# Results written back into their operands' pages, an unscaled first chunk and a new order of steps in a two-layer hybrid encoder

## The chip, the cores and the metric

The kernel runs on one core of a Trainium2 chip. Its engines each work through a list of instructions in the order in which the program gives them: TensorE (PE) multiplies matrices, its weight loads are PEld; VectorE (DVE), ScalarE (ACT) and GpSimd (POOL) do the elementwise work; SyncE (SP) issues nearly all transfers, and ACT a few. Matrix results land in PSUM banks, from where ACT or DVE must copy them before a bank can be used again. The metric is the device time of one execution in microseconds; lower is better. The kernel before takes 1392.69 us (median of three runs, 1391.5 to 1395.56).

## The reference

Two layers over 1024 new frames (eight tiles of 128 rows) and, with the same weights, 32 later frames (a ninth tile) that also read caches. In each layer:

```
h = rmsnorm(x, norm_g);  z = h @ w_in          # 1024 -> 2976 columns, cut into
(a_q, a_k, a_v, a_g,  b_cq, b_ckv, b_kr, b_g,  c_q, c_k, c_v, c_g) = split(z)
ret  = retention(rope(a_q), rope(a_k)/8, a_v)             # 4 heads, chunk by chunk, with a state
q    = [rmsnorm, rope(rmsnorm)] of rmsnorm(b_cq) @ w_uq   # latent attention (MLA), 8 heads of 96
k, v = rmsnorm(b_ckv) @ w_ukv, and one rotated key part for all heads
mla  = softmax(q k^T / sqrt(96), causal by chunks of 64) v
band = softmax(rms(c_q) rms(c_k)^T / 8 + bias[clip(distance)]) c_v   # last 8 chunks and own
mix  = [rmsnorm(ret)*silu(a_g), mla*silu(b_g), band*silu(c_g)]
y    = x + mix @ w_out
```

The outputs are y of both groups and, per layer, the retention state, the normalised latents and the normalised band keys and values.

## The kernel before, in words

Every product that feeds the results is made from two float32r parts, hi and lo: `whi` and `wlo` of a weight, `H_94` (hi) and `H_95` (lo) of the transposed input, and three matmuls (hi*hi, hi*lo, lo*hi) stand for one.

**Pages.** SBUF is cut into 60 pages of 128x512 float32 (`N_PAGES`, L40). `page()` takes the one that has been free longest, `free()` gives it back. Work beside the main line is written as tasks (Python generators): `prep` (input of a tile), `b` (latent attention's q, k, v of a tile), `ret`, `bk`, `bq`, `band`, `smp`, `mla`. A task takes its next step when its input is there, when a clock that the planner keeps has passed its due time (`GAPS`), and when `safe()` finds pages enough for all tasks that have begun (`NEED`, `MOST`, `STREAMS` per kind). So the tables of numbers at the top set the order in which the program is written; a scheduler then orders the instructions of each engine within these dependencies.

**Stages of a layer.** `layer_in` projects the 1024 columns in eleven steps, in the order of `STEPS`: "b" (416 columns), and then 256 columns at a time. The steps ag, bg0, bg1, cg are gates (`gates`), the others run tile by tile (`chunk`): 24 matmuls of one tile into a bank `pj` (there are two), which `unload` copies into a page `z`. The weights of a step are fetched a step ahead. Band attention of two tiles (`band_attn`) runs beside the gates: `band_score` makes 128 rows against up to five key tiles in two banks `s` (there are three), adds the bias, takes the maximum and the exponential (pages `bs` and `bPA`); `transposed` turns the probabilities through banks `ps` (three) into pages `PT`; `values` multiplies them with v. Then come 64 units of latent attention (`mla`: score, transpose, values), beside which the two halves of the output product (`out_part`) run at the rates `RATES`; the second begins no earlier than `STARTS[1]`.

**The start.** In the first layer x comes in transposed already (`xt`, two halves of 256 KB a tile), and the row norm is applied after the product: `first_prep` splits `xt` in `H`, squares it, sums the squares over its columns by a matmul with ones (`s<-ones,xsq`) and takes the power -0.5 (`rstd`, result `r0`). `unload` scales by `r0` as it copies a bank, so a bank waits for the norm of its tile. The tile t=1 is loaded on ACT's queue, all else on SP's. `misc_task` writes the flipped position bias 128 times into DRAM (`bt`, 768 KB, for both layers) and loads it again in slanted rows (`braw`, `braws`).

Of the kernel before, what the change touches and what calls it, by code (L numbers as in the profile page):

```python
# [39 lines left out]
FETCH_B = 20  # L40
E2 = "G"
STEPS = ("b", "ak", "cv", "ck", "av", "aq", "bg0", "cq", "ag", "cg", "bg1")
CAP = 16
AHEAD_U = 8
NEED_W = dict(b=17, u=16)
# [13 lines left out]
MOST = dict(prep=2, misc=2, b=5, ret=4, bk=2, bq=7, band=7, smp=3, mla=4)  # L59
MARGIN = 0  # L60
STREAMS = dict(prep=3, misc=1, b=2, ret=2, bk=1, bq=1, band=2, smp=1, mla=1)
BANKS = dict(ps=3, s=3, pj=2)
# [28 lines left out]
class Task:  # L91


    def __init__(self, kind, gen, when):
        self.kind, self.gen, self.when = kind, gen, when
        self.ready, self.held, self.started = 0.0, 0, False


class Kern:
# [167 lines left out]
    def may(self, task):  # L267
        return self.safe(max(0, min(MOST[task.kind], NEED[task.kind] - task.held)), task)

# [3 lines left out]
    def step_task(self, task):  # L273
        task.started = True
        self.cur, last = task, self.cur
        try:
            with self.urgent(URGENT.get(task.kind, 0)):
                next(task.gen)
# [177 lines left out]
    def prep(self, t, xh, hT):  # L456
        n = 128 if t < 8 else NS
        xn = [self.page([512], name="xn") for _ in range(2)]
        ss = self.st(2)
        for j in range(2):  # L460
            self.act(xn[j][:n], xh[j][:n], AF.Square, scale=1.0 / 32, accum_out=ss[:n, j:j + 1])
# [9 lines left out]
        self.free(*xh)  # L471
        yield
        for j in range(2):
            p = self.bank((4, 128), "prep")
            for i in range(4):
                self.tr(p[:, i, :n], xn[j][:n, 128 * i:128 * i + 128])
            self.parts(t, j, p[:, :, :n], hT)
        self.free(*xn)
        self.prepped.add(t)
        yield  # L480

    def first_prep(self, t, hT):
# [4 lines left out]
        for j in range(2):  # L487
            (self.nc.scalar if t == 1 else self.nc.sync).dma_start(
                xt[j], (A["xt_p"][t] if t < 8 else A["xt_s"])[:, 4 * j:4 * j + 4])
        yield  # L490
        for j in range(2):
            self.parts(t, j, xt[j], hT, LO0[j])
        yield
        for x in xt:
# [11 lines left out]
        self.free(sq)  # L506
        self.prepped.add(t)
        yield
# [15 lines left out]
    def new_hT(self):  # L524
        self.prepped = set()
# [32 lines left out]

    def unload(self, t, p, W, z=None):

        if z is None:
            z = self.page([W], name="z")
        with self.urgent(URGENT_Z):
            if t < 8:
                self.act(z, p, **({} if self.rb is None else dict(scale=self.r0[:, t:t + 1])))
            elif self.rb is None:
                self.unstack(z[:NS], p)
# [6 lines left out]

    def b_task(self, l, t, z):
        A = self.A
        n = 128 if t < 8 else NS
        ss = self.st(3)
        sq = self.page([416], name="sq")
# [17 lines left out]
        self.free(z, sq, kr)  # L597
        yield
# [67 lines left out]
    def q_task(self, l, t, n, ch, cl):  # L666
        for c in range(2):
# [12 lines left out]
            yield  # L680
            qn = self.page([4, 96], name="qn")
            rp = self.page([2, 4, 32], name="rp")
# [9 lines left out]
            else:  # L692
                self.qs[c] = qn
            self.free(rp, zq, sq)
            yield

    def kv_task(self, l, t, n, ch, cl, kr):
# [3 lines left out]
        for c in range(2):  # L701
            p = self.bank((4, 128), "b")
            self.latent(p, ch, cl, [(2, self.W["u"][4 + c])])
            zk = self.page([4, 64], name="zk")
            self.unstack(zk[:n], p[:, :, :64])
# [6 lines left out]
            yield  # L712
            kt = self.page([4, 96], name="kt")
            self.tt(kt[:n, :, :64], zk[:n], r[:n].unsqueeze(2).to_broadcast([n, 4, 64]), OP.mult)
            self.free(zk, sq)
            self.nc.gpsimd.tensor_copy(kt[:n, :, 64:], kr[:, None, :].to_broadcast([n, 4, 32]))
# [203 lines left out]
    def ret_task(self, l, t, zk, zq):  # L920
# [4 lines left out]
        tmp = self.page([2, 4, 2, 32], name="rt")  # L925
        rx = self.page([8, 64], name="rx")
        for j, src in enumerate((zq, zk)):
# [8 lines left out]
        self.free(zq)  # L936
        ro = self.page([8, 2, 32], name="ro")
        self.tt(ro[:n, :, 0], zz[:, :, 0], tm[:, :, 1], OP.subtract)
        self.tt(ro[:n, :, 1], zz[:, :, 1], tm[:, :, 0], OP.add)
        xz = (self.xz if t < 8 else self.xzs)[:n].unsqueeze(2).to_broadcast([n, 8, 64])  # L940
        self.tt(rx[:n], ro[:n].rearrange("p h a d -> p h (a d)"), xz, OP.mult)
        self.free(z, tmp, ro)
        yield
# [112 lines left out]
    def band_k_task(self, l, t, z):  # L1056
# [12 lines left out]
        self.free(z, sq)  # L1069
        if t >= 4:  # L1070
# [56 lines left out]
    def band_prep(self, l, pr):  # L1127
# [27 lines left out]
        for j in range(2):  # L1155
# [6 lines left out]
            self.bqt[2 * pr + j] = (qh, ql)  # L1162
        yield

    def band_attn(self, l, pr):
        b0 = 2 * pr
        yield from self.band_prep(l, pr)
        for b in (b0, b0 + 1):
            q = self.bqt.pop(b)
            PT, sums = [], self.st(4)  # L1170
            for h in range(4):
                P = self.band_score(h, b, q, sums[:, h:h + 1])
                yield
                PT.append(self.transposed(P))
                yield
            o = self.bank((2, 128), "o")
            for hp in range(2):
                self.values(o[:, hp], [(k, self.bv[k][:, 128 * hp:128 * hp + 128])
                                       for k in range(max(0, b - 4), b + 1)], PT[2 * hp:2 * hp + 2])
            p = self.inverse_rows(sums, 2)  # L1180
            mx = self.mixboth(3, b)
            self.put_mix((6, 7), (b,), mx, p)
            self.tt(mx, o, mx, OP.mult)
            yield
            self.bfull = b + 1
            self.free(*q)
# [4 lines left out]

    def band_score(self, h, b, q, so):

# [4 lines left out]
        m = self.st(2)  # L1198
        t = self.page([128 * nb], name="bs")
        sB = self.bank((128 * x + 128,), "s")  # L1200
# [255 lines left out]
    def layer_in(self, l, hT):  # L1456
# [12 lines left out]
        def cb_b(t, p):  # L1469
            self.spawn("b", self.b_task(l, t, self.unload(t, p, 416)), lambda: "u" in self.W)  # L1470
            if t == MISC_T:
# [41 lines left out]
        for name, nxt in zip(STEPS, STEPS[1:] + (None,)):  # L1513
# [5 lines left out]
            for _ in gen(name):  # L1519
# [3 lines left out]
                self.poll()  # L1523
                self.press(lambda: len(self.fg) > CAP or not self.safe(2))
            for x, _ in todo:
# [27 lines left out]
    def run(self):  # L1553
# [17 lines left out]
        self.poll()  # L1571
        self.load(self.tab, A["tab"])
        self.load_layer(0)
        x_of = src_p
        for l in range(DEPTH):
# [33 lines left out]
            for x, _ in enumerate(self.mla(l)):  # L1609
                self.poll()  # L1610
                self.press(lambda: not self.safe(6))
                for i in range(2):
# [67 lines left out]
```

## Time and profile before

| | |
|---|---|
| time, median of 3 runs | 1392.69 us (1391.5 to 1395.56) |
| profiled execution | 1385.13 us, span of the profile 1383.3 us |
| PE busy | 1327.4 us (96%) in 10339 matmuls |
| DVE, ACT, POOL busy | 845.3, 760.5 and 458.9 us (61%, 55%, 33%) |
| the chain that ended last | PE 79%, DMA 7%, ACT 4%, DVE 4%, POOL 4% |
| transfers | 130.56 MB, 94 GB/s over the span |

The busy share of an engine is the time in which it has an instruction in it; PE's instructions overlap, so 96% does not say that PE ran at its peak. The granted clock of PE (PEclk) is given as a share of its full speed: 1.00 is 2.4 GHz, 0.50 is 1.2 GHz. A row of the timeline begins with its start and its duration in us; what stands in brackets behind it is how long the engine had been idle and what ended that.

### The profile page before, as it was taken

The numbers are of one execution on the slowest core, as the hardware profiler recorded it, in microseconds if no ns is written. First come the engines' busy times: TensorE is split into PE (matmuls) and PEld (weight loads), VectorE is DVE, ScalarE is ACT, GpSimd is POOL, SyncE is SP. The second block draws the span as 40 slices with busy tenths as digits, with TensorE's granted clock in tenths as the row PEclk, the third lists the DMA queues.
The fourth block names the chain that finished last, engine by engine and source line by source line (L and its number), as shares of the span: only waits on it lengthen the run. The fifth ranks groups of instructions, "written<-read, shape, count | busy, mean of one in ns | idle before, by whom it ended". The sixth has DMA issues, their size and how long they took to land.

```text
span 1383.3 us, 28562 instructions
## 1 busy us (share of the span) xinstructions
PE 1327.4 (96%) x10339; PEld 1214.6 (88%) x10339; DVE 845.3 (61%) x2558; ACT 760.5 (55%) x2180; POOL 458.9 (33%) x686
## 2 busy tenths in 40 slices
PE   6899999999998999999999999999999999999898
PEld 5899999999898788887889999999989988888787
DVE  7655657666776657565562556665766766656543
ACT  6455545353655757676672445454555576667551
POOL 4656766343000313221122456754320022222110
PEclk9999999999999999999999999999999999999999
DMA  7334341131211433432240344221212133433131
GB/s 250 94 91 149 115 124 37 35 92 36 64 52 34 145 102 117 132 101 89 108 155 12 107 134 132 82 73 32 85 43 77 36 97 112 151 111 113 66 124 65
DMA packets 131077, 130.56 MB, mean 94 GB/s; under 512 B 14392, under 2 KB 107256, under 8 KB 130936
## 3 DMA queue, kind: packets, MB, share of 16 engines
q1 hardware_dynamic: 130648, 128.21, 29.7%
q8 instruction: 81, 1.33, 0.4%
q14 instruction: 60, 0.49, 0.1%
q10 hardware_dynamic: 288, 0.52, 0.1%
HBM read 84.48 MB, written 45.79 MB: 94 GB/s over the span
## 4 chain that ended last, share of the span: by engine, by line
PE 79%; DMA 7%; ACT 4%; DVE 4%; POOL 4%; issue 2%; SPq 0%; ACTq 0%; DVEq 0%; POOLq 0%
PE pj L177 46%; PE s L177 11%; PE ps L177 11%; PE ps L183 8%; DMA raw<-in_w_in 2%; POOL rs L242 2%; PE pj L183 2%; PE s L183 1%; DMA raw<-in_w_out 1%; ACT PT L187 1%; DVE wlo L210 1%; ACT P L187 1%; DMA xt<-in_xt_p 1%; ACT whi L187 1%; POOL ms L203 1%
## 5 line engine op out<-in xcount | busy, mean ns | idle before, releaser
L177 PE MATMUL pj<-whi,H 128*128 128x256 f32 (+1 forms) x1792 | 368.3, 297 | 11.4 <-DVE whi L203 8.6
L177 PEld LDWEIGHTS pj<-whi,H 128*128 128x128 f32 x1792 | 294.7, 192 | 15.4 <-ACT xt L187 8.6
L177 PE MATMUL pj<-wlo,H 128*128 128x256 f32 (+1 forms) x896 | 264.9, 296 | 1.1 <-DVE wlo L210 1.1
L177 PE MATMUL pj<-H,whi 128*128 128x256 f32 (+1 forms) x1024 | 205.4, 293 | 2.7 <-DVE th L210 1.4
L187 ACT ACTIVATE PT<-ps 128x384 f32<-128x384 f32 (+3 forms) x304 | 130.7, 456 | 108.8 <-PE ps L183 103.7
L177 PEld LDWEIGHTS pj<-wlo,H 128*128 128x128 f32 x896 | 171.8, 192 | 3.5 <-DVE wlo L210 2.0
L242 POOL TENSOR_TENSOR rs<-ms,nhalf 128x4 f32<-128x4 f32 (+5 forms) x141 | 164.8, 1169 | 9.3
L177 PEld LDWEIGHTS pj<-H,whi 128*128 128x128 f32 x1024 | 162.9, 191 | 5.5 <-DVE th L210 1.8
L195 POOL TENSOR_TENSOR mlo<-mix,mhi 128x256 fp32r<-128x256 f32 x96 | 69.1, 738 | 275.4 <-ACT mhi L187 159.4
L177 PE MATMUL pj<-H,wlo 128*128 128x256 f32 (+1 forms) x512 | 149.0, 291 | 0.3 <-DVE wlo L210 0.3
L203 POOL TENSOR_SCALAR ms<-st 128x4 f32<-128x4 f32 (+6 forms) x166 | 57.4, 346 | 233.3 <-DVE st L214 194.6
L195 POOL TENSOR_TENSOR wlo<-raw,whi 128x512 fp32r<-128x512 f32 x32 | 40.7, 1280 | 272.5 <-PE ps L183 114.2
L177 PE MATMUL s<-H 96*128 96x384 f32 (+3 forms) x516 | 127.3, 363 | 2.5 <-ACT P L187 2.3
L214 DVE TENSOR_REDUCE st<-s 128x1 f32<-128x384 f32 (+3 forms) x220 | 118.2, 539 | 6.5 <-PE s L177 3.4
L187 ACT ACTIVATE whi<-raw,cols 128x256 fp32r<-128x256 f32 (+2 forms) x178 | 83.4, 516 | 69.3 <-DMA raw<-in_w_in 58.9
L210 DVE SCALAR_TENSOR_TENSOR wlo<-raw,cols,whi 128x256 fp32r<-128x256 f32 (+2 forms) x184 | 91.2, 528 | 42.3 <-ACT whi L187 39.6
L187 ACT ACTIVATE P<-s,st 128x384 f32<-128x384 f32 (+3 forms) x172 | 99.9, 587 | 28.6 <-DVE st L203 27.9
L177 PE MATMUL pj<-whi,mhi 128*128 128x512 f32 x256 | 103.4, 404 | 2.8 <-ACT whi L187 1.9
L177 PE MATMUL pj<-wlo,mhi 128*128 128x512 f32 x256 | 100.8, 394 | 0.0
L177 PE MATMUL pj<-whi,mlo 128*128 128x512 f32 x256 | 100.4, 395 | 0.0
L177 PEld LDWEIGHTS pj<-H,wlo 128*128 128x128 f32 x512 | 98.0, 191 | 1.4 <-DVE wlo L210 0.9
L177 PEld LDWEIGHTS s<-H 96*128 96x128 f32 x516 | 86.2, 192 | 12.7 <-ACT P L187 5.3
(262 smaller groups left out, 2807.0 us busy)
## 6 DMA issues: line engine op xcount, KB each, us to landing
raw<-in_w_in SPq DMA_DIRECT2D x80, 256.0 KB, 3.0
raw<-in_w_out SPq DMA_DIRECT2D x32, 256.0 KB, 3.2
yp<-yres SPq DMA_DIRECT2D x32, 256.0 KB, 2.3
yres<-yp SPq DMA_DIRECT2D x32, 256.0 KB, 2.7
qd<-qn SPq DMA_DIRECT2D x32, 192.0 KB, 1.9
kd<-kt SPq DMA_DIRECT2D x32, 192.0 KB, 2.0
sk<-kd SPq DMA_DIRECT2D x32, 192.0 KB, 3.3
sq<-qd SPq DMA_DIRECT2D x32, 192.0 KB, 2.6
```

Source lines behind the costliest of these rows:

```text
L177: self.nc.tensor.matmul(out, lhsT, rhs, start=start, stop=stop)
L183: self.nc.tensor.transpose(out, in_, self.ident[:k, :k])
L187: r = self.nc.scalar.activation(out, in_, func, **kw)
L195: (self.nc.vector if eng == "D" else self.nc.gpsimd).tensor_tensor(out, a, b, op=op)
L203: (self.nc.vector if eng == "D" else self.nc.gpsimd).tensor_scalar(out, a, s1, s2, op0=op0, **kw)
L210: self.nc.vector.scalar_tensor_tensor(out, a, s, b, op0=op0, op1=op1)
L214: self.nc.vector.tensor_reduce(out, in_, axis=AX.X, op=op, negate=negate)
L242: self.nc.gpsimd.tensor_tensor(r[:n], ms[:n], self.nhalf[:n, :w], op=OP.pow)
```

## The change

1. **In place.** Where a page held only an operand of the last use, the result is written into it: `xn` into x (`prep`), `bn` into `z` (`b_task`), `qn` into `zq`, the normalised key into the page of `kt` (`kv_task`), `rx` and `ro` into `rz` (`ret_task`), `kn` into `z` (`band_k_task`), the transposed probabilities into their own page (`transposed`), and the near scores of two heads share one page (`band_attn`).
2. **First chunk unscaled.** In the step "b" of the first layer `unload` copies the bank without `r0`; `b_task` scales `z` in place afterwards, when the tile's norm is there (`normed`).
3. **First loads.** The tiles 0 and 1 are loaded on ACT's queue; one small load of columns moves behind the table. Of the eight weight blocks of the first step DVE makes `whi` of two (before: six), ACT of six.
4. **Order and tables.** cv and ck are projected straight after b, ahead of ak, av and aq. The needs, gaps, rates and starts have new numbers, and a band step may ask for two pages only.

```
-W0 = 3
+W0 = 1
+SIDE = 2
-RATES = (0.45, 0.4, 0.8)
-SMALL = 4
-STARTS = (2, 40)
+RATES = (0.55, 0.45, 0.7)
+SMALL = 2
+STARTS = (2, 48)
-STEPS = ("b", "ak", "cv", "ck", "av", "aq", "bg0", "cq", "ag", "cg", "bg1")
+STEPS = ('b', 'cv', 'ck', 'ak', 'av', 'aq', 'bg0', 'cq', 'ag', 'cg', 'bg1')
-GAPS = dict(bk=200, bq=300, ret=450)
-GAP = 450
-NEED = dict(prep=4, misc=2, b=10, ret=4, bk=2, bq=7, band=16, smp=3, mla=4)
+GAPS = dict(bk=200, bq=150, ret=450, band=700)
+GAP = 150
+NEED = dict(prep=2, misc=2, b=8, ret=3, bk=1, bq=7, band=14, smp=3, mla=4)
...
-            (self.nc.scalar if t == 1 else self.nc.sync).dma_start(
+            (self.nc.scalar if t < SIDE else self.nc.sync).dma_start(
...
-                self.act(z, p, **({} if self.rb is None else dict(scale=self.r0[:, t:t + 1])))
+                self.act(z, p, **({} if self.rb is None or raw else dict(scale=self.r0[:, t:t + 1])))
...
+        if raw:
+            self.act(z[:n], z[:n], scale=self.r0[:n, t:t + 1])
...
-        bn = self.page([416], name="bn")
+        bn = z
...
-            qn = self.page([4, 96], name="qn")
+            qn = zq
...
-            zk = self.page([4, 64], name="zk")
+            kt = self.page([4, 96], name="kt")
+            zk = kt[:, :, :64]
...
-        kn = self.page([4, 64], name="kn")
+        kn = z[:, :256].rearrange("p (h d) -> p h d", h=4)
...
+                    if not h % 2:
+                        near = self.page([2, 256], name="bs")
+                    P = self.band_score(h, b, q, sums[:, x:x + 1], near[:, h % 2])
+                    yield 2
...
-            d = self.page([e - a, 128], name="PT")
+            d = t.rearrange("p (a b) -> p a b", b=128)
             self.evacuate(d, p, e - a)
-            self.free(t)
...
-        for l in range(DEPTH):
-            self.load(self.lcols[l], A["cols"][l])
+        self.load(self.lcols[0], A["cols"][0])
...
         self.load(self.tab, A["tab"])
+        self.load(self.lcols[1], A["cols"][1])
```

**How instructions move.** On SP, the start of the program, before; `raw` are the weight blocks of "b", `xt` halves of tiles (xt_191 and 192 are tile 2, 248 and 249 tile 3, then tiles 4 and 5), `bt` is the bias table:

```order
L247 DMA raw_177<-in_w_in 128x416
L488 DMA xt_191<-in_xt_p 128x512
L488 DMA xt_192<-in_xt_p 128x512
L247 DMA tab<-in_tab 128x1008
L247 DMA G<-in_gains 128x256
L488 DMA xt_248<-in_xt_p 128x512
L488 DMA xt_249<-in_xt_p 128x512
L488 DMA xt_266<-in_xt_p 128x512
L488 DMA xt_267<-in_xt_p 128x512
L488 DMA xt_317<-in_xt_p 128x512
L488 DMA xt_318<-in_xt_p 128x512
L247 DMA bt_111<-in_bflip 512x1x384
```

The same stretch after the change; tile 3 is now xt_332 and 333, tile 4 xt_336 and 337:

```order
L250 DMA raw_176<-in_w_in 128x416
L492 DMA xt_190<-in_xt_p 128x512
L492 DMA xt_191<-in_xt_p 128x512
L250 DMA tab<-in_tab 128x1008
L250 DMA cols_84<-in_cols 128x16
L250 DMA G<-in_gains 128x256
L250 DMA bt_111<-in_bflip 512x1x384
L492 DMA xt_332<-in_xt_p 128x512
L492 DMA xt_333<-in_xt_p 128x512
L492 DMA xt_336<-in_xt_p 128x512
L492 DMA xt_337<-in_xt_p 128x512
L250 DMA raw_368<-in_w_uq 128x384
```

The bias table stands six loads earlier, ahead of the inputs of the tiles 3 and 4.

On ACT, where the first two banks `pj` of the program are copied to `z`, before:

```order
L187 ACTIVATE H_94<-xt_318 128x4x128
L187 ACTIVATE xt_249<-xt_249 128x512
L187 ACTIVATE xt_266<-xt_266 128x512
L187 ACTIVATE z_264<-pj_223,r_91 128x416
L187 ACTIVATE xt_267<-xt_267 128x512
L187 ACTIVATE z_310<-pj_270,r_91 128x416
```

And after the change:

```order
L190 ACTIVATE xt_191<-xt_191 128x512
L190 ACTIVATE H_94<-xt_332 128x4x128
L190 ACTIVATE z_227<-pj_202 128x416
L190 ACTIVATE z_259<-pj_229 128x416
L190 ACTIVATE H_94<-xt_333 128x4x128
L190 ACTIVATE z_227<-z_227,r_91 128x416
```

The copy no longer reads the norm `r_91`, and right ahead of it stands the split of tile 3's first half, xt_332; the scaling follows as a step of its own.

On PE, at the end of the first layer's gates (`pj<-H,wlo` 128x288 is the last one), band scores (`s<-bk`) and the transposes of their probabilities (`ps<-ident,bPA`, `ps<-ident,bs`), before:

```order
L177 MATMUL pj_6392<-H_94,wlo_5662 128x288
L177 MATMUL pj_6830<-H_95 128x128 x2
L177 MATMUL s_6465<-bk_4171,bqh_5618 128x128
L177 MATMUL s_6465<-bk_4171,bql_5619 128x128
L177 MATMUL s_6465<-bk_4390,bqh_5618 128x256
L177 MATMUL s_6465<-bk_4390,bql_5619 128x256
L177 MATMUL pj_6830<-H_95 128x128
L177 MATMUL s_6534<-bk_5529,bqh_5618 128x256
L177 MATMUL s_6534<-bk_5529,bql_5619 128x256
L177 MATMUL s_6538<-bk_4171,bqh_5618 128x128
```

And after the change:

```order
L180 MATMUL pj_6423<-H_94,wlo_5593 128x288
L186 MATMUL ps_6485<-ident,bPA_6420 128x128 x3
L186 MATMUL ps_6490<-ident,bs_6402 128x128 x2
L180 MATMUL s_6508<-bk_4254,bqh_5510 128x128
L180 MATMUL s_6508<-bk_4254,bql_5511 128x128
L180 MATMUL s_6508<-bk_4481,bqh_5510 128x256
L180 MATMUL s_6508<-bk_4481,bql_5511 128x256
L180 MATMUL s_6524<-bk_5701,bqh_5821 128x256
L180 MATMUL s_6524<-bk_5701,bql_5822 128x256
L186 MATMUL pj_6436<-ident,sq_6313 96x128 x2
```

Of the first layer's band scores 46 matmuls stood behind the last gate before, 22 do now; the others have moved up among the gates.

## Rows read from the trace of the kernel before

**Rows 1.** The page: busy time of two engines, and the slices of PE:

```profile
PE 1327.4 (96%) x10339; PEld 1214.6 (88%) x10339; DVE 845.3 (61%) x2558; ACT 760.5 (55%) x2180; POOL 458.9 (33%) x686
PE   6899999999998999999999999999999999999898
```

**Rows 2.** PE by stretch: stretch, us, PE busy (matmuls), PEclk, DMA share, GB/s:

```profile
0.00:60.00 60.00, 42.25 (x198) 0.91 0.60 192
330.00:470.00 140.00, 129.53 (x1120) 0.96 0.23 67
1010.00:1140.00 130.00, 125.75 (x1150) 0.99 0.21 63
1140.00:1383.00 243.00, 232.86 (x1692) 1.00 0.32 107
```

**Rows 3.** Timeline of PE in the first 47 us:

```profile
8.58 1.03 PE L177 MATMUL pj<-whi,H 128*128 128x416 f32 x2 [8.58 <-DVE whi L203]
...
25.70 0.38 PE L177 MATMUL s<-ones,xsq 128*128 128x1 f32 x2 [3.91 <-DVE xsq L214]
25.94 0.43 PE L177 MATMUL pj<-whi,H 128*128 128x416 f32 x1
...
41.65 0.34 PE L177 MATMUL pj<-whi,H 128*128 128x416 f32 x1
45.94 0.90 PE L183 MATMUL ps<-ident,bn 128*128 128x128 f32 x3 [3.94 <-DVE bn L203]
47.09 0.72 PE L177 MATMUL pj<-whi,H 128*128 128x416 f32 x1 [0.25 <-ACT z L187]
```

**Rows 4.** Timeline of SP, DVE and ACT in the first 46 us:

```profile
2.61 4.71 SPq L247 DMA_DIRECT2D raw<-in_w_in  x8
9.13 0.33 SPq L247 DMA_DIRECT2D G<-in_gains  x1
14.11 0.82 SPq L247 DMA_DIRECT2D bt<-in_bflip  x1
25.17 0.61 ACT L187 ACTIVATE z<-pj,r 128x416 f32<-128x416 f32 x1 [1.92 <-POOL r L242]
28.13 0.63 ACT L187 ACTIVATE H<-xt 128x512 fp32r<-128x512 f32 x1 [0.82 <-DMA xt<-in_xt_p]
31.27 0.68 SPq L247 DMA_DIRECT2D bt<-in_bflip  x1
42.54 0.62 DVE L203 TENSOR_SCALAR bT<-braw 128x256 f32<-128x256 f32 x2 [4.51 <-DMA braw<-bt]
45.53 0.35 DVE L203 TENSOR_SCALAR bn<-z,rs 128x256 f32<-128x256 f32 x1
```

**Rows 5.** The same table of stretches, around the two waits and inside the band stage:

```profile
8.00:10.00 2.00, 1.03 (x2) 1.00 1.06 398
28.00:30.00 2.00, 2.00 (x7) 0.50 0.59 208
48.00:50.00 2.00, 2.00 (x7) 0.50 0.11 33
422.00:426.00 4.00, 4.00 (x39) 0.50 0.56 164
642.00:646.00 4.00, 4.00 (x20) 0.65 0.22 77
```

**Rows 6.** Waits of PE from 330 to 470 us: total, times, longest:

```profile
PE ps L183 <- ACT bPA L187: 2.6, 4, 1.3
PE pj L177 <- ACT whi L187: 2.5, 2, 1.3
PE s L177 <- DVE bs L195: 2.3, 3, 1.2
PE s L177 <- ACT bPA L187: 1.9, 1, 1.9
```

**Rows 7.** Longest wait of PE from 1140 us on:

```profile
PE ps L183 <- ACT P L187: 2.6, 4, 1.4
```

More of the change, by code (lines that the diff above doesn't have):

```diff
@@ L55 @@
 URGENT_MLA = 0
[L56 to L59 removed]
+GAPS = dict(bk=200, bq=150, ret=450, band=700)
+GAP = 150
+NEED = dict(prep=2, misc=2, b=8, ret=3, bk=1, bq=7, band=14, smp=3, mla=4)
+MOST = dict(prep=1, misc=2, b=4, ret=2, bk=1, bq=7, band=7, smp=3, mla=4)
 MARGIN = 0
[L61 removed]
+BAND_GROUPS = ((0, 1),)
+SAFE_IN, SAFE_MLA = 3, 9
+STREAMS = dict(prep=3, misc=1, b=2, ret=3, bk=1, bq=1, band=2, smp=1, mla=1)
 BANKS = dict(ps=3, s=3, pj=2)
@@ L95, in __init__ @@
         self.kind, self.gen, self.when = kind, gen, when
-        self.ready, self.held, self.started = 0.0, 0, False
+        self.ready, self.held, self.started, self.most = 0.0, 0, False, MOST[kind]
 class Kern:
@@ L267, in may @@
     def may(self, task):
-        return self.safe(max(0, min(MOST[task.kind], NEED[task.kind] - task.held)), task)
+        return self.safe(max(0, min(task.most, NEED[task.kind] - task.held)), task)
     def urgent(self, offset):
@@ L277, in step_task @@
             with self.urgent(URGENT.get(task.kind, 0)):
-                next(task.gen)
+                task.most = next(task.gen) or MOST[task.kind]
             task.ready = max(self.clk.values()) + GAPS.get(task.kind, GAP)
@@ L457, in prep @@
         n = 128 if t < 8 else NS
-        xn = [self.page([512], name="xn") for _ in range(2)]
+        xn = xh
+        sq = self.page([512], name="xsq")
         ss = self.st(2)
         for j in range(2):
-            self.act(xn[j][:n], xh[j][:n], AF.Square, scale=1.0 / 32, accum_out=ss[:n, j:j + 1])
+            self.act(sq[:n], xh[j][:n], AF.Square, scale=1.0 / 32, accum_out=ss[:n, j:j + 1])
         s1 = self.st(1)
@@ L492, in first_prep @@
             self.parts(t, j, xt[j], hT, LO0[j])
+        self.prepped.add(t)
         yield
@@ L506, in first_prep @@
         self.free(sq)
-        self.prepped.add(t)
+        self.normed.add(t)
         yield
@@ L712, in kv_task @@
             yield
-            kt = self.page([4, 96], name="kt")
             self.tt(kt[:n, :, :64], zk[:n], r[:n].unsqueeze(2).to_broadcast([n, 4, 64]), OP.mult)
-            self.free(zk, sq)
+            self.free(sq)
             self.nc.gpsimd.tensor_copy(kt[:n, :, 64:], kr[:, None, :].to_broadcast([n, 4, 32]))
@@ L925, in ret_task @@
         tmp = self.page([2, 4, 2, 32], name="rt")
-        rx = self.page([8, 64], name="rx")
+        rx = z.rearrange("p j h a d -> p (j h) (a d)")
         for j, src in enumerate((zq, zk)):
@@ L936, in ret_task @@
         self.free(zq)
-        ro = self.page([8, 2, 32], name="ro")
-        self.tt(ro[:n, :, 0], zz[:, :, 0], tm[:, :, 1], OP.subtract)
-        self.tt(ro[:n, :, 1], zz[:, :, 1], tm[:, :, 0], OP.add)
+        self.tt(zz[:, :, 0], zz[:, :, 0], tm[:, :, 1], OP.subtract)
+        self.tt(zz[:, :, 1], zz[:, :, 1], tm[:, :, 0], OP.add)
         xz = (self.xz if t < 8 else self.xzs)[:n].unsqueeze(2).to_broadcast([n, 8, 64])
-        self.tt(rx[:n], ro[:n].rearrange("p h a d -> p h (a d)"), xz, OP.mult)
-        self.free(z, tmp, ro)
+        self.tt(rx[:n], rx[:n], xz, OP.mult)
+        self.free(tmp)
         yield
@@ L1169, in band_attn @@
             q = self.bqt.pop(b)
[L1170 to L1184, printed above, removed]
+            for hps in BAND_GROUPS:
+                m = len(hps)
+                PT, sums = [], self.st(2 * m)
+                for x, h in enumerate(range(2 * hps[0], 2 * hps[0] + 2 * m)):
+                    if not h % 2:
+                        near = self.page([2, 256], name="bs")
+                    P = self.band_score(h, b, q, sums[:, x:x + 1], near[:, h % 2])
+                    yield 2
+                    PT.append(self.transposed(P))
+                    yield 2
+                o = self.bank((m, 128), "o")
+                for x, hp in enumerate(hps):
+                    self.values(o[:, x], [(k, self.bv[k][:, 128 * hp:128 * hp + 128])
+                                          for k in range(max(0, b - 4), b + 1)], PT[2 * x:2 * x + 2])
+                p = self.inverse_rows(sums, m)
+                mx = self.mixboth(3, b)[:, hps[0]:hps[0] + m]
+                self.put_mix([6 + hp for hp in hps], (b,), mx, p)
+                self.tt(mx, o, mx, OP.mult)
+                yield 2
             self.bfull = b + 1
@@ L1198, in band_score @@
         m = self.st(2)
-        t = self.page([128 * nb], name="bs")
+        t = t[:, :128 * nb]
         sB = self.bank((128 * x + 128,), "s")
@@ L1469, in cb_b @@
         def cb_b(t, p):
-            self.spawn("b", self.b_task(l, t, self.unload(t, p, 416)), lambda: "u" in self.W)
+            self.spawn("b", self.b_task(l, t, self.unload(t, p, 416, raw=True), self.rb is not None),
+                       lambda: "u" in self.W and (self.rb is None or t in self.normed))
             if t == MISC_T:
@@ L1523, in layer_in @@
                 self.poll()
-                self.press(lambda: len(self.fg) > CAP or not self.safe(2))
+                self.press(lambda: len(self.fg) > CAP or not self.safe(SAFE_IN))
             for x, _ in todo:
@@ L1610, in run @@
                 self.poll()
-                self.press(lambda: not self.safe(6))
+                self.press(lambda: not self.safe(SAFE_MLA))
                 for i in range(2):
```

23 lines of the change are left out of this document (11 added, 12 removed).

## The prediction

> **What bounds the kernel now.** I read the page first: PE is busy for 1327.4 of 1383.3 us, and the dips stand in the first two slices and near the slices 11 to 14 [rows 1]. So there are some 56 us to be had at most, and every other engine (61%, 55%, 33%) matters only through what it makes PE wait for. The table of stretches then says where those 56 us lie [rows 2]: 17.8 us in the first 60 us (60 - 42.25), 10.5 us in 330 to 470 (the first layer's band attention, and the change of stages behind it), 4.3 us in 1010 to 1140 (the same stage of the second layer), and 10.1 us from 1140 on. In the first and second of these the granted clock is also below full (0.91 and 0.96), so PE loses there twice. The timeline of the start [rows 3, 4] and the list of waits of the band stage [rows 6] say what it waits for. The change leaves every matmul as it is; it can only move these gaps.
>
> **The start, first matmul.** The first weight block is issued at 2.61 [rows 4] and PE begins at 8.58 [rows 3]. With both tiles on ACT's queue and one small load less in front, four issues leave SP ahead of it, so it is issued about 1.4 us sooner, and DVE makes two of the eight `whi` instead of six (0.6 us each). Tiles 0 and 1 will be through the array some microseconds earlier. I cost this at nothing all the same, because of what decides the start of tile 2. From 8 to 10 us the transfers run at 398 GB/s, full in their share (1.06) [rows 5], so the second queue changes who lands first, hardly when all has landed. The Trainium skill, page DMA: Bandwidth & Descriptors, section Issuing engines are not separate DMA queues, says the same in general: a second issuing engine saves issue time only, since all share 16 DMA engines. By that rule alone the start would gain those 1.4 us of issue and no more.
>
> **Tile 2.** Before, PE stands 3.91 us for the norm sum ahead of tile 2 and begins it at 25.94 [rows 3]; the bank of tile 0 is copied at 25.17, when its norm is there [rows 4]. The unscaled copy takes this wait away. What is late next is read from the order: the copy of tile 0's bank now stands on ACT behind the split of tile 3's first half, and tile 3's loads stand on SP behind the bias table. Tile 2 needs that bank, since there are two. What a load behind that table costs is in the trace twice: the table is issued at 14.11 and the half tile behind it is usable at 28.13, 14.0 us later; the second table is issued at 31.27 and `braw` behind it is usable at 42.54, 11.3 us later [rows 4]. After the change the table follows G directly, which was issued at 9.13 [rows 4], so at about 9.5. Tile 3 is then usable between 20.8 and 23.5; I take 23.5, since it is the same table in the same crowded queue. With 0.63 for the split and 0.61 for the copy [rows 4] tile 2 starts at 24.7 (22.0 at the other end), 1.2 us earlier (3.9). Against it stands the clock: behind each of the two waits PE ran at 1.2 GHz for some microseconds (28 to 30 and 48 to 50 at 0.50 [rows 5]). As tiles 0 and 1 end sooner and tile 2 hardly does, PE idles here for about twice the 3.9 us, and I add 0.5 us (up to 2.7) for a longer slow stretch. Net 0.7 us gained, bounds 3.9 gained and 1.5 lost.
>
> The Trainium skill, page DMA: Bandwidth & Descriptors, section Rules for kernel authors, has a rule that speaks against moving this table forward: an outermost dimension below 16 confines a DMA to as many engines, and the table's is 4 (heads). A load spread over all 16 then waits for the four slow ones; the 14.0 and 11.3 us agree, and nothing in the sum rests on it.
>
> **Tile 5.** Before, PE ends tile 4 at 41.99 and stands 3.94 us for `bn`, then 0.25 for the bank [rows 3]. DVE could not make `bn` (45.53) because ahead of it stood the bias, whose `braw` was waiting behind the second table [rows 4]. In the new program `braw` is issued ahead of the second table, so DVE has done the bias long before. The wait goes, and so does its slow stretch: from 47.09 to about 51 tile 5 ran at half speed [rows 3, 5], 4 us of which half is lost. 3.94 + 0.25 + 2.1 = 6.3 us gained; nothing, if another load takes the place of `braw`.
>
> **Tile 6.** That other load exists: tile 6's halves now stand behind the second table. I reckon that table issued at 34 to 35, and the halves usable 11.3 us later, at 46; tile 6 is wanted at about 46. I add 1 us, bounds 0 and 4. The start as a whole: -0.7 - 6.3 + 1.0 = -6.0 us.
>
> **Band stage, first layer.** Of the 10.5 us idle, 2.6 + 1.9 + 2.3 us are waits for the exponential (`bPA`) and for the bias sum (`bs`) [rows 6]: a few band scores follow one another with nothing between that PE could do, and the third must wait for a bank or the transposes for ACT. 2.5 us are a late weight. On top, a clock of 0.96 over 140 us is 5.6 us [rows 2], as from 422 to 426, where PE is busy throughout at half speed [rows 5]. The new program needs fewer pages (a band task 14 instead of 16, b 8 instead of 10), starts its band steps sooner, and puts 22 instead of 46 band matmuls behind the last gate. More gate matmuls between a score and its use cover the same latency. Of some 15 us I take a third, 5 us; bounds 10 gained, and 4 lost where a moved step makes a gap that I don't see. **Second layer**: idle 4.3 us and 0.01 of 130 us of clock [rows 2], 5.6 together, of which I take 1.5 (4 gained, 2 lost).
>
> **Latent attention and output.** In place a transpose's result goes to a page that PE has just read; the copy already had to wait for those transposes, so no wait is added. Rates and starts: 18 turns of the first half at 0.40 to 0.45 ended after some 46 units, at the new 0.45 to 0.55 after some 41, while the second half begins at 48. So some five units more per layer run with no output matmuls between them. Where PE waits in this stage, it is for the exponential `P`, 4 times in 243 us, at most 1.4 us [rows 7]. I add 1.5 us, bounds -2 and +7.
>
> **What costs nothing.** Nine scalings of 0.61 us are added on ACT (5.5 us), four `whi` move to it (2.5 us); ACT is busy 55% [rows 1], and the scalings stand in a stretch where it waits for loads. If that cover were gone they would delay a tile's q and k, up to 1 us. Retention, now denser (three tasks instead of two): 0, bounds 3 each way. Fewer pages taken issue no instruction.
>
> **Sum.** -6.0 - 5.0 - 1.5 + 1.5 = -11.0 us. The profiled execution took 1385.13 us (span 1383.3), so it would take 1374.1; the runs' median stands 7.6 us above the profiled one, and I keep that distance: 1392.69 - 11.0 = 1382 us.
>
> **The rivals.**
> *The whole gap closes.* Tile 3 comes at the early end (-3.9, with -6.3 and no wait at tile 6: -10.2), the band stages give back their bounds (-10 and -4): -24 us, 1368. For it: the clock losses vanish with the gaps that cause them, so gains come in pairs. Against: nothing in the order takes the bank limit of three `s` away.
> *Given back.* The two bias tables hold the start after all (tile 2 +1.5, tile 6 +4, against -6.3), and the band's gaps only move: about -1 us, 1392. For it: both tables stand ahead of inputs now; against: before, one of them stood ahead of `braw`, and that is gone.
> *Slower: latent attention runs dry.* The ten units (five a layer) that lose their output matmuls each wait for `P`: up to 1.4 us [rows 7], and after a long wait the clock falls (642 to 646 at 0.65, 1.4 us of 4 lost [rows 5]), 2.5 us a unit. -12.5 + 25 makes 1405. It decides from 1.7 us a unit on, where it exceeds all else by 4 us. For it: this stage has the shortest chain of work beside it; against: before, some such units were there already and all waits for `P` of the second layer's stage are 2.6 us [rows 7].
>
> **How the numbers follow.** I give the forecast 0.54, the closed gap 0.20, given back 0.15, slower 0.11. About 4 us (0.3%) is what a measurement of this kernel can tell from no change. The forecast's own range is 1374 to 1389; the closed gap lies below, both faster. So faster 0.73, same 0.15 and slower 0.12. The range for 8 in 10 is 1364 to 1394: it leaves out the slow case and a little at the low end.
>
> **What would show it.** Right: tile 2 starts at 22 to 25 us, after an idle time of PE of some 8 us that a load on ACT ends; no wait for the key latent (now `z`) near 42; tile 6 starts before 50; PE in the first 60 us busy for some 48 us; waits for `bPA` and `bs` at half in the first layer's band stage. Wrong: a wait of PE for `H` of the tiles 3 or 6 over 10 us; waits for `P` between unit 40 and 48 of each layer over 1.5 us; or the first 60 us no better than before.

## The result, and the profile after

The changed kernel took 1371.3 us (median of 4 runs, 1368.29 to 1373.05); the kernel before, run beside it on the same chip, 1392.1 us (1386.21 to 1395.56). The ratio is 0.9853, 95% interval 0.9814 to 0.9891: faster by 1.5%. The forecast was 1382 us, its range 1364 to 1394. The sign and the range held, the size was half of what came.

Of the profiled executions, 1385.13 us became 1370.73, 14.4 us less. The page's row of busy times, after [rows 1]:

```profile
PE 1325.1 (97%) x10339; PEld 1215.1 (89%) x10339; DVE 843.5 (62%) x2549; ACT 767.5 (56%) x2196; POOL 459.1 (34%) x686
```

The matmuls are the same 10339, and PE is idle for 43.8 us instead of 55.9. ACT does 7.0 us more (the scalings and the `whi` it took over; 8.0 were costed, and hidden). The table of stretches of after; columns are stretch, us, PE busy (matmuls), PEclk, DMA share, GB/s. The rows from 24 and from 34 us are the start of tile 2 and a stretch about 2 us behind the second bias table's issue:

```profile
0.00:60.00 60.00, 45.76 (x208) 0.91 0.60 192
24.00:26.00 2.00, 1.31 (x4) 0.50 0.92 304
34.00:36.00 2.00, 2.00 (x13) 1.00 0.25 94
330.00:470.00 140.00, 133.71 (x1168) 0.99 0.26 76
1010.00:1140.00 130.00, 129.17 (x1154) 1.00 0.28 82
1140.00:1368.00 228.00, 219.97 (x1602) 0.99 0.31 100
```

Against [rows 2] the first 60 us gained 3.5 us of busy time, the first layer's band stretch 4.2 and 0.03 of clock, the second layer's 3.4; from 1140 on PE is idle for 8.0 us instead of 10.1.

Since both programs make the same matmuls, the k-th matmul of a kind (projection, latent attention, output) can be looked up in both timelines. How far after is ahead of before at these marks (times of before in brackets), stage by stage:

| up to | after minus before, us | this stage alone | forecast of it |
|---|---|---|---|
| the start, and the steps up to 184 us | -2.0 | -2.0 | -6.0 |
| end of the first layer's gates (439 us) | -7.7 | -5.7 | -5.0 |
| second layer begins (716 us) | -7.5 | +0.2 | part of +1.5 |
| end of the second layer's gates (1122 us) | -8.4 | -0.9 | -1.5 |
| end | -14.4 | -6.0 | part of +1.5 |

Part of the last -6.0 is work that moved ahead of the mark: behind the second layer's gates 18 matmuls fewer are left, and PE is busy for 244.7 us instead of 247.3 and idle for 9.8 instead of 13.2. Behind the first layer's gates 77 matmuls fewer are left, and PE is idle for 16.5 us instead of 12.1; its waits for `P` there rose from 2.2 to 6.3 us, the longest from 0.8 to 1.3.

The start as it is now, PE's timeline (start, us, operation, and in brackets the idle time before it and what ended it):

```profile
6.09 0.69 PE L180 MATMUL pj<-whi,H 128*128 128x416 f32 x1 [6.09 <-ACT H L190]
...
24.69 0.71 PE L180 MATMUL pj<-whi,H 128*128 128x416 f32 x1 [4.20 <-ACT z L190]
...
41.20 0.44 PE L180 MATMUL pj<-whi,H 128*128 128x416 f32 x1
...
49.37 0.38 PE L180 MATMUL s<-ones,xsq 128*128 128x1 f32 x2 [2.24 <-DVE xsq L217]
49.61 0.57 PE L180 MATMUL pj<-whi,H 128*128 128x416 f32 x1
...
50.76 1.06 PE L180 MATMUL pj<-whi,H 128*128 128x416 f32 x2 [0.23 <-DVE H L198]
```

These rows are the first matmul, the start of tile 2, that of tile 5, the norm sum of tile 5 (which stands ahead of tile 6 in PE's order), the start of tile 6, and its third matmul, which waits for the low parts of its input. The wait for `bn` ahead of tile 5 [rows 3] is gone; in its place stands one ahead of tile 6. What lies behind both waits is on SP and ACT in the same trace:

```profile
10.31 0.81 SPq L250 DMA_DIRECT2D bt<-in_bflip  x1
...
23.47 0.63 ACT L190 ACTIVATE H<-xt 128x512 fp32r<-128x512 f32 x1 [4.09 <-DMA xt<-in_xt_p]
24.12 0.93 ACT L190 ACTIVATE z<-pj 128x416 f32<-128x416 f32 x2
...
32.25 0.68 SPq L250 DMA_DIRECT2D bt<-in_bflip  x1
33.03 2.89 SPq L250 DMA_DIRECT2D raw<-in_w_in  x2
...
43.76 0.91 ACT L190 ACTIVATE whi<-raw,cols 128x256 fp32r<-128x256 f32 x2 [3.48 <-DMA raw<-in_w_in]
44.58 0.62 ACT L190 ACTIVATE xt<-xt 128x512 f32<-128x512 f32 x1
...
45.90 0.61 ACT L190 ACTIVATE H<-xt 128x512 fp32r<-128x512 f32 x1
```

The half tile behind the first bias table is usable 13.2 us after the table's issue, and ACT, which would copy the bank for tile 2, stands 4.09 us in front of it. The weight behind the second table is usable 10.7 us after its own issue, ACT stands 3.48 us for that one, and the square of tile 5's second half (44.58) and tile 6's splits (45.90) stand behind it. DVE sums that square at 48.28, and PE, which has ended tile 5 at 46.09, waits for the sum. Tile 6's own halves had landed at 45.04 and 46.39.

PE's waits (total, times, longest) in the first layer's band stretch, after [rows 6]:

```profile
PE s L180 <- DVE bs L198: 2.8, 2, 2.0
PE ps L186 <- ACT bPA L190: 2.5, 2, 1.3
```

And the longest of after from 1140 us on [rows 7]:

```profile
PE ps L186 <- ACT P L190: 2.9, 4, 1.4
```

### The profile page after: what moved, and what is told of

The parts are those of the page before. It is cut to its first block, busy times and chain, and to the rows that moved or that the text cites. A ratio compares the mean times of both kernels' runs of the same rounds, so it can differ in the third digit from the quotient of the medians.

```text
span 1368.9 us, 28603 instructions
## 1 busy us (share of the span) xinstructions
PE 1325.1 (97%) x10339; PEld 1215.1 (89%) x10339; DVE 843.5 (62%) x2549; ACT 767.5 (56%) x2196; POOL 459.1 (34%) x686
## 4 chain that ended last, share of the span: by engine, by line
PE 50%; ACT 3%; DVE 2%; DMA 1%; issue 1%; POOL 1%; ACTq 0%; DVEq 0%
PE pj L180 30%; PE ps L180 7%; PE s L180 6%; PE ps L186 5%; ACT P L190 1%; PE pj L186 1%; PE s L186 1%; DMA raw<-in_w_in 1%; ACT whi L190 0%; ACT xsq L190 0%; DVE st L217 0%; DVE wlo L213 0%; POOL rs L245 0%; DMA raw<-in_w_out 0%; DMA bqt<-bd 0%
## 5 line engine op out<-in xcount | busy, mean ns | idle before, releaser
L245 POOL TENSOR_TENSOR rs<-ms,nhalf 128x4 f32<-128x4 f32 (+5 forms) x141 | 168.2, 1193 | 8.7
L190 ACT ACTIVATE P<-ps 128x384 f32<-128x384 f32 (+2 forms) x192 | 89.7, 490 | 75.9 <-PE ps L186 74.8
L180 PE MATMUL s<-H 96*128 96x384 f32 (+3 forms) x486 | 121.6, 368 | 1.2 <-ACT P L190 1.2
L217 DVE TENSOR_REDUCE st<-s 128x1 f32<-128x384 f32 (+3 forms) x210 | 112.2, 536 | 6.3 <-PE s L180 4.5
L206 POOL TENSOR_SCALAR ms<-st 128x4 f32<-128x4 f32 (+5 forms) x166 | 55.3, 333 | 167.0 <-DVE st L217 146.7
L190 ACT ACTIVATE P<-s,st 128x384 f32<-128x384 f32 (+2 forms) x162 | 94.4, 588 | 20.4 <-DVE st L206 18.7
L186 PE MATMUL ps<-ident,P 128*128 128x128 f32 x576 | 89.8, 276 | 7.8 <-ACT P L190 7.4
L186 PEld LDWEIGHTS ps<-ident,P 128*128 128x128 f32 x576 | 69.9, 141 | 20.2 <-ACT P L190 11.3
```

The source lines that it names most:

```text
L180: self.nc.tensor.matmul(out, lhsT, rhs, start=start, stop=stop)
L186: self.nc.tensor.transpose(out, in_, self.ident[:k, :k])
L190: r = self.nc.scalar.activation(out, in_, func, **kw)
L206: (self.nc.vector if eng == "D" else self.nc.gpsimd).tensor_scalar(out, a, s1, s2, op0=op0, **kw)
L217: self.nc.vector.tensor_reduce(out, in_, axis=AX.X, op=op, negate=negate)
L245: self.nc.gpsimd.tensor_tensor(r[:n], ms[:n], self.nhalf[:n, :w], op=OP.pow)
```

## The experiments

My theory after the result: the start gained only 2 us because the two bias tables hold what stands behind them; the rest comes from the pages, which let the new numbers run tasks earlier. Each kernel below computes the full result. "Ratio" is to the kernel before on the same chip, with its 95% interval.

**e1: the table in another form.** Edit of after; the copies stand outermost, not the four heads:

```
-        self.load(bt, bass.AP(..., ap=[[384, 4], [0, 128], [1, 384]]))
+        self.load(bt.rearrange("h p c -> p h c"), bass.AP(..., ap=[[0, 128], [384, 4], [1, 384]]))
```

> The changed kernel with one edit: the bias table is written to DRAM with the 128 copies as the outermost dimension of the transfer (before: the 4 heads); every instruction stays where it was. If the table holds the start, as predicted: the half tile behind it is usable some 4 to 6 us sooner than 23.5, tile 2 starts at 19 to 21 instead of 24.7 and tile 6 no longer waits at 47 to 50.8; 6 to 9 us faster than the changed kernel, about 1364. Rival (the queue is full anyway and the shape of one transfer changes nothing): tile 2 at 24 to 25, within 2 us of 1371.

Measured: 1362.36 us, ratio 0.982 (0.9794 to 0.9846), span 1358.0. Its table of stretches, the first 60 us, a stretch about 2 us behind the second table's issue, and the one with the longest wait:

```profile
0.00:60.00 60.00, 49.17 (x250) 1.00 0.60 195
30.00:32.00 2.00, 2.00 (x14) 1.00 1.10 334
40.00:44.00 4.00, 1.14 (x7) 1.00 0.05 16
```

Its timeline, the second table, the weight behind it, and the wait ahead of tile 6:

```profile
28.27 0.59 SPq L250 DMA_DIRECT2D bt<-in_bflip  x1
28.96 1.09 SPq L250 DMA_DIRECT2D raw<-in_w_in  x2
...
35.59 0.91 ACT L190 ACTIVATE whi<-raw,cols 128x256 fp32r<-128x256 f32 x2 [0.97 <-DMA raw<-in_w_in]
...
42.92 0.38 PE L180 MATMUL s<-ones,xsq 128*128 128x1 f32 x2 [2.64 <-DVE xsq L217]
```

The order of the instructions is the same as in after on every engine. The weight behind the table is usable 6.6 us after its issue instead of 10.7; tile 2 has no wait and starts at 20.47, tile 6 starts at 43.16, and the clock stays at 1.00. That tile 6 would no longer wait did not come true: PE still stands 2.64 us for tile 5's norm sum, only earlier. The marks are 7.5 us ahead of after's at 95 us, 9.3 where the second layer begins, and 10.9 at the end. So the table's form was what held the start. What this is worth in the median is less sure: before took 1387.01 us beside e1 and 1392.1 beside after, and by the ratios e1 is 4.6 us ahead of after, with intervals that overlap.

**e2: after with the start of before** (W0, the two queues, the scaled copy, the columns' load):

```
-W0 = 1
-SIDE = 2
+W0 = 3
...
-                self.act(z, p, **({} if self.rb is None or raw else dict(scale=self.r0[:, t:t + 1])))
+                self.act(z, p, **({} if self.rb is None else dict(scale=self.r0[:, t:t + 1])))
```

> The changed kernel with the start as before (norm applied as the bank is copied, tile 0 on SP's queue, six whi on DVE, both column loads first); all else of the change stays. If the start brings what the two traces show at tile 6, 3 us: about 1374. Rival (the start is worth more than that, since the runs differ by 20.8 us and the profiles by 14.4 only): 1380 or more.

Measured: 1366.52 us, ratio 0.9849 (0.9825 to 0.9873). PE's timeline has the old wait for the norm sum and a small one ahead of tile 5:

```profile
25.33 0.59 PE L179 MATMUL s<-ones,xsq 128*128 128x1 f32 x2 [3.86 <-DVE xsq L216]
...
44.43 0.59 PE L185 MATMUL ps<-ident,z 128*128 128x128 f32 x3 [1.80 <-DVE z L205]
```

The edits of the start are worth nothing measurable here (0.9849 and 0.9853); with the slow table they exchange one wait for another. In the traces tile 7 starts at 54.42 us with the old start and at 59.09 with the new one.

**e8: e2 with e1's table.**

> The changed kernel with the start as before, and the bias table in 128 outer copies. With the slow table the new start was worth nothing (1366.5 without it, by a ratio of 0.9849 against 0.9853 with it). If the table hid what it brings, the old start with the fast table keeps the wait for the norm sum ahead of tile 2 and is 4 to 6 us behind the new start with the fast table (span 1358.0): span about 1363. Rival (the new start brings nothing at all): span 1356 to 1360.

Measured: 1364.45 us, ratio 0.9835 (0.981 to 0.986), span 1364.2, near the theory's. Tile 7 starts at 53.46 us here and at 51.56 in e1.

**e9: the kernel before with e1's table and nothing else.**

> The kernel before with one edit: the bias table's copy has its 128 copies outermost instead of its 4 heads. Theory (the table's copy held the loads behind it, and the start of before waits only in part for them, as e8 against e2 showed with 2.1 us): the 4.5 us wait of ACT for braw and the 3.9 us wait of TensorE for bn become under 1 us, TensorE's busy time in the first 60 us rises from 42.3 to at least 45, and the time is 3 to 7 us below that of before (1385 to 1389 if before is 1392). Rival (those waits were from the place of the loads in the queue, not from the table's form): waits as before, time within 2 us of before.

Measured: 1383.52 us, ratio 0.9967 (0.9947 to 0.9987), which is 4.6 us. In its timeline of PE the wait ahead of tile 2 stays, as it is one for the norm, and `bn` comes without a wait [rows 3]:

```profile
25.38 0.59 PE L177 MATMUL s<-ones,xsq 128*128 128x1 f32 x2 [3.86 <-DVE xsq L214]
...
42.64 0.49 PE L183 MATMUL ps<-ident,bn 128*128 128x128 f32 x3
```

PE is busy for 47.30 us of the first 60, and the wait of 4.5 us for `braw` [rows 4], which is DVE's and not ACT's, is gone. So the 3.94 us that tile 5 lost before were the table's doing. What the new start is worth beside a fast table stays open: e8 and e1 lie 6.2 us apart in their spans and 2.1 in their medians, with intervals that overlap.

**e12: e1, with the table issued at tile 4** (`MISC_T = 4`).

> The kernel after with the bias table's copy in 128 outermost copies (as in e1) and issued with tile 4 instead of tile 2. Theory (with that form the table costs only its own 16-engine time, about 2 us, and no wait behind it is left): same as e1 within 2 us, 1360 to 1365. Rival (what is left of the wait for the first tiles' norms, 2.6 us at 42.9 us, comes from the table's share of the loads): 1 to 3 us below e1.

Measured: 1363.69 us, ratio 0.9818 (0.9787 to 0.9849), as e1 within the intervals. The wait of 2.64 us for the norm sum is gone in it and PE is busy for 50.88 us of the first 60, but the time is no shorter: with this form the table's place gives nothing more that can be measured.

**e3: after with all old numbers** (tables of needs, gaps, rates, starts and the order of steps; in place and the new start stay), and **e4: before with in place alone**, old numbers, old start:

```
-        xn = [self.page([512], name="xn") for _ in range(2)]
+        xn = xh
...
-            qn = self.page([4, 96], name="qn")
+            qn = zq
```

> The changed kernel with the numbers and the order of steps of before (needs, gaps, rates, starts, steps, streams); in-place results and the new start stay. If room for pages brings the gain in the band and attention stages: 1371 to 1375. Rival (the new numbers and the order of steps bring it, and in-place results only allow them): about 1385, with the first layer's stretch from 330 to 470 idle for 8 us or more again.

> The kernel before with the in-place results alone (numbers, order of steps and start as before). If room for pages brings the gain: 1377 to 1381, 11 to 15 us faster than before. Rival (the numbers and the order bring it): 1389 to 1392.

Measured: e3 1411.31 us, ratio 1.0174 (1.0147 to 1.0202); e4 1410.97 us, ratio 1.0163 (1.0137 to 1.019). Both lie above all that was expected. In place alone makes the kernel slower by 1.6%: the theory that more room in the pages is a gain by itself fell, and so did the rival's place for the loss, as PE is idle for only 6.5 us from 330 to 470 us in e3 (10.5 in before). The chain of waits of e4 in the first layer's projections (start, us, what):

```profile
72.04 2.05 DMA qd<-zq
74.11 0.38 ACT kt L189
74.50 0.28 ACT vp L189
...
83.93 0.38 SPq L252
84.37 2.85 DMA raw<-in_w_in
87.25 0.05 issue
87.30 0.52 ACT whi L189
```

A store of a page on which the result was left (`zq`) is, in this chain, waited for by the next copies on ACT; some steps later a weight's fetch leaves SP only behind another store, and `whi` waits for it. Added up over the whole chains, weights of `in_w_in` and stores `qd` stand in it for 50.4 and 19.5 us; in the chain of before for 32.1 and 5.1.

**e5: before with the new numbers alone** (order of steps, gaps, rates, starts, three streams; own pages, old needs, old start):

```
-RATES = (0.45, 0.4, 0.8)
+RATES = (0.55, 0.45, 0.7)
...
-GAPS = dict(bk=200, bq=300, ret=450)
-GAP = 450
+GAPS = dict(bk=200, bq=150, ret=450, band=700)
+GAP = 150
```

> The kernel before with the new order of steps, gaps, rates, starts, streams and fetch points, but with results in pages of their own, the old needs per task and the old start. In-place results with the old numbers took 1411 (1.6% slower). If the new numbers bring the gain whatever the pages: 1370 to 1378 (0.985 to 0.99). If numbers and pages only work together: 1385 to 1400, no faster than before.

Measured: 1409.43 us, ratio 1.0161 (1.0125 to 1.0197). It lies above both ranges. At 394 us (in the first layer's last gate) this kernel is level with before, after having been 13 us behind at 213 us: so the new numbers gain some 13 us in the band stretch, and without the pages they lose that ahead of it, and where the second layer begins they are 15 us behind. From 60 to 210 us PE waits for copies of its banks that it does not wait for in after:

```profile
PE pj L177 <- ACT z L187: 3.1, 1, 3.1
PE pj L177 <- ACT zk L187: 2.1, 1, 2.1
```

**e6, e7, e10, e11: one group of after's numbers put back each.** e6 the reservations (`NEED`, `MOST`, two streams, `yield` without 2), e7 the gaps, e10 the order of the steps, e11 the latent attention's numbers:

```
e6  -NEED = dict(prep=2, misc=2, b=8, ret=3, bk=1, bq=7, band=14, smp=3, mla=4)
    +NEED = dict(prep=4, misc=2, b=10, ret=4, bk=2, bq=7, band=16, smp=3, mla=4)
e7  -GAP = 150
    +GAP = 450
e10 -STEPS = ('b', 'cv', 'ck', 'ak', 'av', 'aq', 'bg0', 'cq', 'ag', 'cg', 'bg1')
    +STEPS = ('b', 'ak', 'cv', 'ck', 'av', 'aq', 'bg0', 'cq', 'ag', 'cg', 'bg1')
e11 -STARTS = (2, 48)
    +STARTS = (2, 40)
```

> The changed kernel with the old needs per task (band 16 for 14, b 10 for 8, ret 4 for 3, prep 4 for 2), the old two retention streams and band steps that may ask for seven pages. If the 40 us between old and new numbers come from tasks that are held back by needs that are no longer true: 1395 to 1411. Rival (from the gaps or the order): 1371 to 1376.

> The changed kernel with the old gaps between a task's steps alone (450 ns by default for 150, band without its 700). If the 40 us come from the gaps: 1395 to 1411, with later steps of b in the stretch 60 to 210. Rival (needs or order): 1371 to 1376.

> The kernel after with the old order of steps alone: the projections of a (ak) stand ahead of those of the band (cv, ck). Theory (the band's keys and values projected early are what lets the band's work of a layer begin early): the gain of about 6 us in the first layer's band stage and 6 in the second's goes, the rest stays: 1378 to 1386. Rival (the gaps and the reservations make the gain, the order of these steps is not what decides): 1368 to 1374. A third outcome, above 1390, would say that reservations and order are tuned to each other as tables and pages were.

> The kernel after with the old numbers of the latent attention alone (rates .45, .4, .8, small 4, starts 2 and 40, 6 safe pages). Theory (the 5 us that the second layer's latent attention and output gained came from these numbers): the milestones up to 430 us stay within 1 us of after, the loss appears behind 1140 us, and the time is 1374 to 1380. Rival (the 5 us came from banks and pages that come free sooner): 1368 to 1373.

Measured, with ACT's wait for weights of `in_w_in` from 60 us on as the list of waits gives it:

| kernel | us | ratio (95%) | total, times, longest |
|---|---|---|---|
| before | 1392.1 beside after | 1 | 58.2, 38, 4.2 |
| after | 1371.3 | 0.9853 (0.9814 to 0.9891) | 32.7, 32, 2.9 |
| e6, old reservations | 1402.03 | 1.0105 (1.0077 to 1.0133) | 50.4, 35, 4.4 |
| e7, old gaps | 1395.42 | 1.0059 (1.004 to 1.0079) | 53.2, 36, 5.0 |
| e10, old order of steps | 1386.25 | 0.9989 (0.9969 to 1.0009) | 59.3, 39, 5.8 |
| e11, old latent attention | 1383.66 | 0.9965 (0.9944 to 0.9985) | 33.3, 33, 2.9 |
| e4, in place alone | 1410.97 | 1.0163 (1.0137 to 1.019) | 65.8, 44, 4.2 |
| e5, new numbers alone | 1409.43 | 1.0161 (1.0125 to 1.0197) | 41.2, 36, 3.2 |

Each group, put back by itself, costs 1.1 to 2.5% of the time (the difference of the ratios), 7.1% together, where the whole change brought 1.5%: the parts do not add. (The numbers `FETCH_B`, `AHEAD_U` and `SAFE_IN` were not put back by themselves.) The times of e6 and e7 lie in the ranges of their theories. Late weights go with the loss in e4, e6, e7 and e10; in e5 and e11 they do not, so they are one way to lose and not the only one.

In e7 the largest single loss lies at the end of the first layer's keys; PE's waits from 200 to 340 us:

```profile
PE ps L186 <- DVE kt L198: 8.6, 1, 8.6
PE s L186 <- DVE roc L198: 4.1, 1, 4.1
```

In e10 the median stands just above the theory's range (1378 to 1386). By the ratios the loss is 1.4%, some 19 us where the theory gave 12: before took 1386.83 us beside it, and all that the change had brought is gone, as in the third outcome. The place is another, too: 10.4 of the 11.8 us that the first layer loses are lost by 250 us, ahead of the first band score, and from there through the whole band stage the distance to after stays at 11.8. So the early projection of the band's keys pays in the projections, beside which ACT's weights come in time; that these are the cause is not shown.

In e11 the time lies above both ranges. The loss is 14.1 us of span; 2.2 of it are there in the first 63 us, where nothing was edited, and 9.4 come behind the second layer's gates, 5.8 of these as waits of PE, most of them for `P`. The output's weights are late there; ACT's waits from 1100 us on, e11:

```profile
ACT whi L190 <- DMA raw<-in_w_out: 12.1, 6, 5.1
```

and after:

```profile
ACT whi L190 <- DMA raw<-in_w_out: 4.8, 5, 2.3
```

## Why the prediction was right in sign and half in size

**First matmul.** 1.4 us earlier was forecast, 2.5 came (three loads leave SP ahead of the first weight, not four; it is issued at 1.19 instead of 2.61). Tiles 0 and 1 end 1.3 us earlier, and that brought next to nothing, for the reason given: tile 2.

**Tile 2.** Start forecast at 24.7, measured 24.69, with a load on ACT ending the idle time and the clock at 0.50 behind it. The price of a load behind the bias table, taken from [rows 4], was right: 14.0 us there, 13.2 here. That the start fits to a hundredth is luck: the table was issued at 10.31 instead of 9.5, which makes up for the price. The idle time ahead of tile 2 was 4.20 us, not some 8.

**Tile 5.** The wait for `bn` went: from the start of tile 4 to that of tile 5 PE takes 4.9 us instead of 9.9, where 4.2 less were forecast, and the clock is at 1.00 behind it, which were the other 2.1.

**Tile 6, the step that failed in the start.** The halves were to be usable at 46, and they landed at 45.04 and 46.39. But I priced only these halves, and the second table held the weight ahead of them as well. ACT stood for that weight, so the square of tile 5's second half came only at 44.58, and PE, ready at 46.09 but for three transposes, stood for tile 5's norm sum until 49.37. Tile 6 starts at 49.61, 3.5 us after it was wanted, and its third matmul waits for the low parts until 50.76. From 44 to 54 us PE is busy for 7.04 us at a clock of 0.83, so the term was 3.0 idle and 1.7 of clock, 4.7 us where I took 1, past its bound of 4. With it my own steps give -2.3 for the start; -2.0 was measured.

The rule that I named as speaking against this change was borne out. The Trainium skill, page DMA: Bandwidth & Descriptors, section Rules for kernel authors, says that an outermost dimension below 16 confines a DMA to at most as many engines. The runs agree: about 2 us behind the second table's issue the mean share of the 16 engines is 0.25 in after (34 to 36 us) and 1.10 in e1 (30 to 32 us), and the load behind the first table lands 12.3 us after its issue in after and 7.8 in e1.

**First band stage.** -5.0 forecast, -5.7 measured between the marks at 184 and 439 us. The waits for `bPA` fell from 4.5 to 2.5 us and the late weight of 2.5 us is gone; the wait for `bs`, which I also expected at half, rose from 2.3 to 2.8. The clock recovered from 0.96 to 0.99. One of my grounds did not hold: the band steps do not start sooner, the first band score comes at 303.8 us instead of 293.8.

**Second layer up to its gates' end.** -1.5 forecast, -0.9 measured.

**Latent attention and output.** +1.5 forecast, -5.8 measured (+0.2 and -6.0): wrong in sign, and past the bound of -2. I counted units that would have no output matmuls beside them and asked only what `P` costs there. The longest wait for `P` from 1140 us on is 1.4 us as before, so nothing ran dry and the slower rival fell; in the first layer the waits for `P` did grow by 4.1 us. What I left out are the band matmuls that no longer stand behind the gates, and what the same numbers do to this stage of the second layer: put back alone (e11), they cost 9.4 us there. By what way is open. The output's weights are late in e11 (12.1 us of waits on ACT), but in before, which has the old numbers too, ACT waits for them for 7.0 us only.

**The rest at nothing.** "Fewer pages taken issue no instruction" is true and misses the point: the reservations and the pages decide which task may start. e3 to e7 show that they had to change together, and a sum of separately priced parts cannot show that. Here it did no harm to the sign, because the change did put them together.

**From the trace to the median.** Of the 10.4 us by which 1381.7 missed 1371.3, 3.4 are terms of the sum (-11.0 for -14.4) and 7.0 are the distance from profile to median that I carried over: 7.6 us then, 0.6 in the kernel after. In 23 later runs the median of before is 1386.83 us, 1.7 above its profiled execution, and 1387.01 and 1386.68 beside e1 and e5, on three chips. So the first three runs stood high; whether by chance or by their chip is open, and after was not run again beside the later ones.

**The rivals.** 1371.3 lies nearest to "the whole gap closes" (1368), but not by its terms: tile 2 did not gain 3.9, tile 6 did not come without a wait, and the second band stage did not give 4. "Given back" was half right: the tables did hold the start.

**The better version.** e1 and e12 are 1.8% below before, each beside its own. Their medians lie 8.9 and 7.6 us below after's, but were not taken beside it; by the ratios it is 4.6 and 4.9 us, with intervals that overlap.

**The signs.** The start of tile 2, the missing wait near 42 us and tile 6 before 50 came as named. The idle time of 8 us was 4.20, the 48 us of busy time in the first 60 were 45.76, and the waits for `bs` did not halve.

## What to carry to other kernels

Price a step from the end of the whole chain that its data pass through, not from the moment the first piece lands: tile 6's input was there on time and the tile 3.5 us late, as another tile's norm sum stood ahead of it. When a load is moved ahead of inputs, first ask what its form costs those behind it; here, beside that one access pattern, the new start was worth nothing measurable, and the pattern cost the kernel before 4.6 us (1.8 to 7.4) too. Where pages, reservations, gaps and the order of steps are tuned together, test the change as a whole before any part of it: in place alone and the new numbers alone each made this kernel 1.6% slower, and the whole change made it 1.5% faster.

## What the runs showed of the hardware

A copy of 786 KB with an outermost dimension of 4 held the load behind it for 12.3 us (its issue at 11.17, landed at 23.44); the same bytes with 128 outermost for 7.8 us (10.82 to 18.62), in the same place of the queue. After PE's idle time of 4.2 us ahead of tile 2 the granted clock was 0.50, the 1.2 GHz level, from 24 to 28 us; in e1 it stayed at 1.00, the 2.4 GHz level, through a stretch of 4 us in which PE was busy for 1.14 us. So the table also cost the slow stretch behind the wait.
